# First head of a hybrid mLSTM/HGRN2 step: both halves of the key weights made in the hand-written order, the gate rows' exponentials moved among the value products, two fill steps moved between queries and scores

## The chip, the cores and the metric

The kernel runs on one core of one Trainium2 chip. The metric is device microseconds of the whole program, lower is better. The engines are named as in the profile: PE multiplies matrices (PEld loads its stationary operand), DVE, ACT and POOL work on tiles, SP issues most of the DMAs.

## The reference, cut to what matters

One layer over 32 new frames of a running stream and 512 frames of a new one (544 columns in all, 1024 features). The branch concerned here is the mLSTM branch, with four heads of 512 features:

```python
xn = _rmsnorm(h, norm_g[l]); proj = xn @ w_in[l]          # u, v, z, input and forget gates, ...
c = silu(causal_conv(u))
qm, km = c @ w_qm[h], (c @ w_km[h]) * M_HD ** -0.5        # per head, 512 x 512
lf = log_sigmoid(fg_pre + b_fg);  b = cumsum(lf)
logd = where(causal, b[t] - b[s] + ig[s], -inf)
m_t = maximum(m_prev, max(logd));  dmat = exp(logd - m_t)
s = (q @ k.T) * dmat                                       # the scores
num = w_inter * (C @ q) + s @ v                            # C, n, m are carried
hm = (layernorm(num / den) + skip * c) * silu(z);  ya = hm @ w_brm
```

The other branch (HGRN2), the merge, the output projection and a per-layer embedding follow. They are not touched.

## The kernel before, in words

Everything is float32, and every product is made of three: each operand is split into a high part `h` (ACT copies it, rounded) and a low part `l` (DVE, or POOL where `eng=G` is given, subtracts), and PE sums high·high, high·low and low·high. So a weight piece of 128x512 needs a DMA into a raw buffer (`wr`, 8 of them), an ACT copy at L132 and a subtraction at L133, and it occupies one of **five** pairs of piece buffers (`wh`/`wl`, `NPIECE`) from then until PE has read it last. `weight(...)` makes two such pieces (`wk000`, `wk001` are the two of the first half of head 0's key weights, `wk010`, `wk011` those of the second half, `wq...` those of the query weights).

The columns are worked in two halves of 272. A dense product of 128 outputs takes 24 or 48 matmuls into two PSUM buffers of a ring of four (`pd`).

**Order.** The opening of the kernel stands in a block in which PE, ACT and DVE keep the order as written: first input units, convolutions, gates, then eight rounds of value products (`vp`, L1396, round k using the pieces `wv k`), with the normalisation of the eight feature tiles (`norm` at L1287/L1290 and `norm_low` at L1294) and the splits of the next weights between them; after the rounds `value_out` empties the four value accumulators (`vh` by ACT at L1317, `vl` by DVE at L1318). After that block only PE keeps its written order. ACT, DVE, POOL and SP get their instructions from a planner that takes the earliest in program order among those it thinks ready. `tc.high_priority()` puts an instruction ahead, and `tc.issue_after(x)` keeps instructions behind x on x's engine.

**Fill.** `Pump` holds independent products (the "fill") and deals them out in steps, so that PE has work while the head's chain of dependent stages goes on. For head 0 the fill is four units `One` (z gate tiles, `wi32` to `wi35` in the profile; 4 blocks of 2 steps each) and two pairs `Two` (the next head's inputs; `wa...`, `ws...`): 60 steps in all. Block i's weights are split by `pump.prepare`, which runs `AHEAD` = 3 blocks ahead of the steps. `pump.limit` is a cap on the blocks that may be prepared. `pump.behind` makes later splits go behind a given instruction.

**Head 0 before the change.** After the rounds: values emptied, remaining norms, splits for blocks 4 and 6 (unit `wi33`), the first half of the key weights `wk00` (low parts on POOL), the last norms, and then the second step of the generator `stage_gates`: on the forget rows (4x544) a DVE operation (L726), an Exp (L727) and an Ln (L728) on ACT. Then PE runs 16 fill steps (`EARLY`: the units `wi32` and `wi33`; in them the weights of unit three, `wi34`, are split), the third step of `stage_gates` (cumulative sums and maxima on DVE, L733 to L754), `stage_k` (its second half of weights, `wk01`, is made there), the last step of `stage_gates` (Exps at L756 to L761, and the rows written to DRAM as `nm_d`), half of `stage_q`, the sums `xf_sums` for k = 0 and 3 (L329 to L341, DVE and ACT), `stage_cols` (rows turned into columns, L782), `stage_decay` (`nm_d` read back as `bc`, masks added at L804, Exp at L810 into `dm`), the other half of `stage_q`, `stage_scores` (`sc`, L881, multiplied by `dm` at L889), and `mchain`: four blocks of keys transposed (`kt`) with one fill step ahead of each, one ahead of the small transposition `kts` (L976), three more, the memory and value products (`C`, `nm`), 20 fill steps, four output transpositions (`yt`), what is left of the fill, and `stage_br` (`ya`, operands `hm`, weights `wbm`).

Of the kernel before, what the change touches and what calls it, by code (L numbers as in the profile page):

```python
# [53 lines left out]
EARLY = 16  # L54
# [12 lines left out]
def hybrid_step(ctx: ExitStack, tc: tile.TileContext, a, o):  # L67
    nc = tc.nc
    V, S, G, PE = nc.vector, nc.scalar, nc.gpsimd, nc.tensor
# [55 lines left out]
    made = {}  # L125
# [11 lines left out]
    def weight(src, name, cols=1024, eng=V, chunk=WP):  # L137

        raws = [(raw_piece(src[:, c : min(c + WP, cols)], f"{name}r{c}"), min(WP, cols - c)) for c in range(0, cols, WP)]
        return [split_piece(r, f"{name}{i}", n, chunk, eng) for i, (r, n) in enumerate(raws)]  # L140
# [157 lines left out]
    st8 = [dict(ub=[], cc=[], cs=[], vt=[], z=[]) for _ in range(MH)]  # L298
# [525 lines left out]
    def stage_k(h):  # L824

        cs = st8[h]["cs"]
        kf, ks = [], []
        for u in range(2):
            w = st8[h].pop("wk", None) or weight(a["w_km"][h, u], f"wk{h}{u}", eng=V if h else G)
            for f in range(2):  # L830
                acc = dense(w, f * P, 256, P, cs, f"k{h}{u}{f}")
                t = eslot(f"kf{h}{u}{f}")
                for b in range(2):
                    read = S.mul(t[:, half(b)], acc[b], HD**-0.5)  # L834
                if u == 0:
                    first = read
                kf.append(t)
                kh, kl = slot(f"kh{h}{u}{f}", F32R), slot(f"kl{h}{u}{f}", F32R)
                S.copy(kh[:, :NP], t[:, NS:T])
                V.tensor_tensor(kl[:, :NP], t[:, NS:T], kh[:, :NP].bitcast(F32), ALU.subtract)  # L840
                ks.append((kh, kl))
        ksm, copied = triple(kf, "ksm")
        st8[h].update(kf=kf, ks=ks, ksm=ksm, copied=copied)
        return first
# [111 lines left out]
    def mchain(h, pump):  # L956
# [5 lines left out]
        for b in range(NB):  # L962
# [7 lines left out]
                S.mul(kh[:, :HD], pt[:, 0, :], wc)  # L970
                V.scalar_tensor_tensor(kl[:, :HD], pt[:, 0, :], wc, kh[:, :HD].bitcast(F32), ALU.mult, ALU.subtract)
            kw.append((kh, kl))
        yield 4 if h else 1
        pt = paux(f"kts{h}")
        for f in range(KH):
            PE.transpose(pt[: 3 * NS, 0, f * P : (f + 1) * P], ksm[:, f], ident)  # L976
# [206 lines left out]
    def hgrn_bounds(decayed):  # L1183

        l0, l1 = vec[:, V_LB : V_LB + HH], vec[:, V_LB + HH : V_LB + 2 * HH]
        lm, le = small("lbm", [P, HH]), small("lbe", [P, 2, HH])
        V.tensor_tensor(lm, l0, l1, ALU.max)
        V.tensor_tensor(le[:, 0, :], l0, lm, ALU.subtract)
        V.tensor_tensor(le[:, 1, :], l1, lm, ALU.subtract)
        with tc.issue_after(decayed.ins):  # L1190
            S.activation(le, le, AF.Exp)

        def rest():
            V.tensor_tensor(lm, le[:, 0, :], le[:, 1, :], ALU.add)
            V.reciprocal(lm, lm)
            V.tensor_tensor(lb, le[:, 0, :], lm, ALU.mult)
            V.tensor_tensor(lc, le[:, 1, :], lm, ALU.mult)

        return rest
# [17 lines left out]
    with tc.manual_schedule(engines={mybir.EngineType.Activation, mybir.EngineType.DVE, mybir.EngineType.PE}):  # L1217
# [62 lines left out]
        def value_weight():  # L1280
            k = len(wv)
            wraw.append(raw_piece(a["w_v"][k], f"wv{k}r"))
            wv.append(split_piece(wraw[k], f"wv{k}"))

        def norm(k):
            t = xt[k]
            V.scalar_tensor_tensor(t[:, :T], t[:, :T], t[:, T : T + 1], rb[:, :T], ALU.mult, ALU.mult)  # L1287
            xh = cp.tile([P, T], F32R, name=f"xh{k}")
            xl = cp.tile([P, T], F32R, name=f"xl{k}")
            S.copy(xh, t[:, :T])  # L1290
            xs.append((xh, xl))

        def norm_low(k):
            return V.tensor_tensor(xs[k][1], xt[k][:, :T], xs[k][0].bitcast(F32), ALU.subtract)  # L1294
# [14 lines left out]
        def value_out():  # L1309
            b = len(vv0)  # L1310
            if b < 2:
                vhl = sp.tile([P, 2, SLOT], F32R, tag="d", name=f"vhl0{b}", bufs=2)
                vh, vl = vhl[:, 0], vhl[:, 1]
            else:
                vh, vl = eslot(f"vh0{b}", F32R), eslot(f"vl0{b}", F32R)
            c = r[:, b + 1 : b + 2]
            S.mul(vh[:, :HD], vp[b], c)  # L1317
            V.scalar_tensor_tensor(vl[:, :HD], vp[b], c, vh[:, :HD].bitcast(F32), ALU.mult, ALU.subtract)  # L1318
            with tc.issue_after(summed.ins):
                G.tensor_copy(vh[:, HD:VW], one4)  # L1320
                G.tensor_copy(vl[:, HD:VW], zero4)
            vv0.append((vh, vl))
# [41 lines left out]
        pump = Pump(fill(0))  # L1364
        for k in range(KD):
            if k == 1:
                conv_rest(3, uin[3], cv[3])
                silu()
                silu_low(2)
                silu()  # L1370
                fg, ig = (slot(n)[:MH, :T] for n in ("fg", "ig"))
                V.tensor_tensor(fg, gt[0:MH, :T], rb[0:MH, :T], ALU.mult)
                V.tensor_tensor(ig, gt[32 : 32 + MH, :T], rb[32 : 32 + MH, :T], ALU.mult)
                gates = stage_gates(fg, ig)
                next(gates)
                value_weight()
                silu_low(3)
                norm(0)
                norm(1)
            if k == 2:  # L1380
                value_weight()
                norm_low(0)
                norm_low(1)
                norm(2)
                value_weight()
                norm(3)
                norm_low(2)
                pump.prepare(1)
                norm_low(3)
                pump.prepare(3)  # L1390
            wh, wl = wv[k]
            xh, xl = x0[k]
            three = ((xh, wh), (xl, wh), (xh, wl))
            for b in range(NB):
                for j, (x, w) in enumerate(three):
                    PE.matmul(  # L1396
                        vp[b],
                        x[:, NS + b * P : NS + (b + 1) * P],
                        w,
                        start=(k == 0 and j == 0),  # L1400
                        stop=(k == KD - 1 and j == 2),
                    )
            if k % NB == NB - 1:
                for j in range(NB):
                    i = k + 1 - NB + j
                    PE.matmul(vq[j * NS : (j + 1) * NS, 0, :], xg[:, i], wraw[i], start=(i < NB), stop=(i >= NB))

        value_out()
        value_out()
        norm(4)  # L1410
        value_out()
        value_out()
        norm_low(4)
        norm(5)
        pump.prepare(5)
        vsum = slot("vsum")[:NS, :HD]
        S.copy(vsum, vq[:NS, 0, :])
        for j in range(1, NB):
            V.tensor_tensor(vsum, vq[j * NS : (j + 1) * NS, 0, :], vsum, ALU.add)
        pump.prepare(7)  # L1420
        st8[0]["wk"] = weight(a["w_km"][0, 0], "wk00", eng=G)
        norm_low(5)
        vs0 = small("vs", [3 * NS, VW], F32R, bufs=1)
        for i in (0, 2):
# [7 lines left out]
        norm(7)  # L1432
        norm_low(6)
        st8[0]["last"] = norm_low(7)
        next(gates)
    with tc.manual_schedule(engines={mybir.EngineType.PE}):
        for h in range(MH):
            if h:
                stage_decay(h)
            else:  # L1440
                st8[0].update(vv=vv0, vs=vs0, cc=cc, cs=cs)
                pump.to(EARLY)
                with tc.issue_after(st8[0]["copies"][0].ins):
                    next(gates)
            stage_k(h)
            if h == 0:

                st8[0]["wq"] = weight(a["w_qm"][0, 0], "wq00")
                with tc.issue_after(made["wq001"][0].ins), tc.issue_after(made["wk011"][1].ins):
                    *_, (nm_d, *rows) = gates  # L1450
            stage_q(h, 0)
            if h == 0:
                with tc.issue_after(st8[0]["last"].ins):
                    for k in (0, 3):
                        xf[k] = xf_sums(k)
                col, cols, combo = stage_cols(*rows)
                stage_decay(h)
                lower_bounds = hgrn_bounds(st8[0]["decayed"])
            low = stage_q(h, 1)
            if h == 0:  # L1460
                pump.behind = low
            else:
                pump = Pump(fill(h))
                pump.to(2)
            low = stage_scores(h)
            if h == 0:
                pump.pairs = low
                with tc.issue_after(low.ins):
                    lower_bounds()
            pump.run(mchain(h, pump))  # L1470
            pump.end()
            if h < MH - 1:
                last = stage_br(h)
            if h == 0:
                with tc.issue_after(last.ins):
                    lmask, smask = level_masks()
# [311 lines left out]
    with tc.manual_schedule(engines={mybir.EngineType.PE}):  # L1788
        pump = Pump(list(units()))
# [36 lines left out]
    for f in range(KD):  # L1826
        w = weight(a["w_brh"][f], f"wbh{f}")
# [182 lines left out]
```

## Time and profile before

| | us |
|---|---|
| median of 3 runs | 1127.63 (1126.51 to 1128.89) |
| the profiled execution, its own time | 1126.18 |
| its span, first to last instruction | 1124.3 |
| busy PE / DVE / ACT / POOL in the span | 1110.2 / 898.3 / 670.7 / 165.3 |
| mean granted TensorE clock | 0.997 |

A row of the timeline gives start, duration, engine, line, operation, output and inputs, and behind it in brackets the idle time of the engine just ahead and what ended it. `x2` is two instructions merged in one row. Matmul durations overlap, so the pace of PE is read from the starts.

### The profile page before, as it was taken

To read this page: it belongs to the slowest core of one execution; us is meant where nothing else is said; L and a number is where in the kernel's file an instruction comes from. 1 tells how busy PE (TensorE), PEld (TensorE's weight loads), DVE (VectorE), ACT (ScalarE), POOL (GpSimd) and SP (SyncE) were. 2 spreads that over 40 slices of the span, in tenths; PEclk is the share of its full clock that TensorE was granted. 3 is DMA by queue.
4 is the path that set the end of the run, shared out by engine and by line. 5 is a ranking of instruction groups with operands and counts; after the bars stand their busy time and mean duration, and the time that the engine had idled before them with its cause. 6 is when DMAs were issued, how large, how long until landed. Compare 5 with 4: busy or idle time off the path is not lost.

```text
span 1124.3 us, 23764 instructions
## 1 busy us (share of the span) xinstructions
PE 1110.2 (99%) x8733; PEld 1086.6 (97%) x8733; DVE 898.3 (80%) x2040; ACT 670.7 (60%) x1505; POOL 165.3 (15%) x308
## 2 busy tenths in 40 slices
PE   9998999999999999999999999999999999999998
PEld 8888999999999999999999999999999999999998
DVE  7888978677797685986888789999999977654485
ACT  6677446754666464665556477777676667333462
POOL 7212000100020000200110123232232210000000
PEclk9998999999999999999999999999999999999999
DMA  6133224423354132542667665666665685332753
GB/s 227 58 122 108 95 76 135 136 66 128 122 169 154 50 124 102 174 167 78 191 190 237 191 146 139 141 133 156 149 148 141 160 225 157 116 103 72 260 155 118
DMA packets 90139, 157.94 MB, mean 140 GB/s; under 512 B 10148, under 2 KB 17828, under 8 KB 90024
## 3 DMA queue, kind: packets, MB, share of 16 engines
q1 hardware_dynamic: 80352, 139.33, 38.4%
q0 software_dynamic: 8784, 15.99, 9.2%
q8 instruction: 68, 1.11, 0.4%
q10 hardware_dynamic: 888, 1.12, 0.3%
q14 instruction: 47, 0.39, 0.1%
HBM read 131.49 MB, written 24.91 MB: 139 GB/s over the span
## 4 chain that ended last, share of the span: by engine, by line
PE 90%; DVE 4%; DMA 3%; ACT 1%; issue 1%; POOL 1%; SPq 0%; ACTq 0%; POOLq 0%; DVEq 0%
PE d L502 36%; PE ya L167 8%; PE yb L167 4%; PE o L167 4%; PE pg L1857 4%; PE k L167 4%; PE q L167 4%; PE C L921 4%; PE nm L1096 3%; PE sc L881 3%; PE pl L1629 2%; PE vp L1396 2%; PE u L287 2%; DMA ws<-in_w_in 2%; PE d L387 1%
## 5 line engine op out<-in xcount | busy, mean ns | idle before, releaser
L420 POOL DMA_DIRECT2D ws<-in_w_in x46 | 40.7, 891 | 235.2 <-DVE hkq L1653 32.1
L516 ACT COPY t<-d 128x272 f32<-128x272 f32 x126 | 47.9, 380 | 8.7 <-PE d L502 8.7
L1653 DVE TENSOR_TENSOR hkq<-hkq,q 128x288 f32<-128x288 f32 (+1 forms) x96 | 40.9, 433 | 3.0 <-PE pl L1637 1.0
L1629 PE MATMUL pl<-hkq,km 128*128 128x128 f32 x224 | 37.7, 290 | 0.6 <-ACT km L1618 0.5
L651 DVE SCALAR_TENSOR_TENSOR cv<-ub,vec,cv 128x547 f32<-128x547 f32 x48 | 37.6, 784 | 0.4
L1629 PEld LDWEIGHTS pl<-hkq,km 128*128 128x128 f32 x224 | 31.1, 189 | 2.2 <-ACT km L1618 1.9
L1618 ACT COPY km<-hkq 128x256 f32<-128x256 f32 x56 | 24.1, 430 | 14.6 <-DVE hkq L1653 4.4
L1030 DVE SCALAR_TENSOR_TENSOR c<-c,wi,Cs 128x258 f32<-128x258 f32 x32 | 15.3, 479 | 18.9 <-PE Cs L1028 18.3
L933 ACT COPY Co<-C 128x258 f32<-128x258 f32 x30 | 9.8, 378 | 31.8 <-PE C L921 29.5
L1174 DVE TENSOR_TENSOR y<-ya,y 128x272 f32<-128x272 f32 x48 | 18.9, 435 | 8.7 <-PE ya L167 8.6
L1660 DVE COPY_PREDICATED at<-lmask,pl 128x256 f32<-128x256 uint8 (+1 forms) x56 | 25.3, 452 | 0.1
L643 POOL COPY uo<-ub 128x3 f32<-128x3 f32 x16 | 17.9, 1119 | 36.1 <-DVE ub L525 27.0
L1107 ACT COPY y<-nm 128x516 f32<-128x516 f32 x16 | 9.5, 591 | 22.9 <-PE nm L1096 22.4
L1597 POOL TENSOR_SCALAR_AFFINE_SELECT aa<-at 128x128 f32<-128x128 f32 x32 | 19.6, 644 | 8.1 <-DVE at L1660 8.0
L1084 DVE BATCH_NORM_STATS2 bs<-y 128x6 f32<-128x512 f32 (+1 forms) x20 | 13.8, 690 | 8.6 <-ACT y L1107 8.3
L821 POOL COPY vsm<-vt 128x96 f32<-128x96 f32 x12 | 6.8, 565 | 88.2 <-DVE vt L523 45.3
L477 POOL DMA_DIRECT2D ws<-in_w_in x15 | 15.5, 1034 | 28.5 <-DVE ws272l L133 24.2
L1096 PE MATMUL nm<-vhl,sh 128*128 128x258 f32 x112 | 18.4, 286 | 0.6 <-ACT y L1107 0.6
L1844 DVE TENSOR_TENSOR h<-o,h 128x272 f32<-128x272 f32 x16 | 6.3, 437 | 14.5 <-PE o L167 14.5
L895 ACT CAST sh<-dm 128x512 fp32r<-128x512 f32 (+3 forms) x16 | 7.4, 461 | 17.2 <-DVE dm L889 17.1
L821 POOL COPY ksm<-kf 128x96 f32<-128x96 f32 x16 | 8.5, 532 | 60.7 <-ACT kf L834 60.7
L1759 ACT ACTIVATE osq<-kq 128x128 f32<-128x128 f32 x32 | 9.8, 307 | 12.4 <-DVE kq L1754 12.1
(4495 smaller groups left out, 4996.0 us busy)
## 6 DMA issues: line engine op xcount, KB each, us to landing
ws<-in_w_in POOLq DMA_DIRECT2D x61, 256.0 KB, 4.7
ws<-in_w_in SPq DMA_DIRECT2D x46, 256.0 KB, 3.4
ya_d<-y SPq DMA_DIRECT2D x32, 272.0 KB, 2.5
y<-ya_d SPq DMA_DIRECT2D x24, 272.0 KB, 3.3
c<-in_C SPq DMA_DIRECT2D x16, 258.0 KB, 3.7
out_Cs<-c SPq DMA_DIRECT2D x16, 258.0 KB, 2.9
out_Cp<-Co SPq DMA_DIRECT2D x12, 258.0 KB, 2.4
x<-in_xT SPq DMA_DIRECT2D x8, 272.5 KB, 4.6
```

What stands on the lines that cost most here:

```text
L167: PE.matmul(both[b][:m, :TH], part(w, off + k * step, m, x), xx[:, half(b)], start=(k == 0 and j == 0), stop=(k == n - 1 and j == 2),)
L420: G.dma_start(t, w_in[u][:, i * WP : (i + 1) * WP], accum_op=ALU.add)
L502: PE.matmul(ps, ww[:, c], xx, start=(start and k == 0 and j == 0), stop=end, skip_group_check=not start,)
L516: self.kept = S.copy(t, ps)
L651: V.scalar_tensor_tensor(cv[:, :547], ub[:, j : j + 547], vcol(V_CW + 4 * ft + j), cv[:, :547], ALU.mult, ALU.add)
L881: PE.matmul(pn[:, 0, :n], ks[f][x][:, j * P : (j + 1) * P], qs[f][y][:, NS + j * P : T], start=(f == 0 and i == 0), stop=(f == KH - 1 and ...
L921: PE.matmul(pn[g][:, :VH], kw[b][x][:, f * P : (f + 1) * P], vv[b][y][:, g * VH : (g + 1) * VH], start=(b == 0 and j == 0), stop=(b == NB ...
L1096: PE.matmul(pn[:, g, :VH], st[j][x][:, (i - j) * P : (i - j + 1) * P], vv[j][y][:, g * VH : (g + 1) * VH], start=(j == 0 and q == 0), stop ...
L1629: PE.matmul(pn[:, 0, b * P : (b + 1) * P], km[:, b * P : (b + 1) * P], view(qq, b * P, ((2 * c, P // (2 * c)), (HB + c, 2), (1, c))), star ...
L1653: V.tensor_tensor(x, x, d, ALU.mult)
L1660: V.copy_predicated(at[:, :n], lmask[:, li, :n], pn[:, 0, :n])
L1857: PE.matmul(ps, part(w, k * P, P, x), xx[:, c], start=(k == 0 and j == 0), stop=(k == KD - 1 and j == 2))
```

## The change

It does five things, all for head 0.

1. The second step of `stage_gates` (L726 on DVE, Exp and Ln on ACT) is written ahead of the last value weight `wv7` in round 2, and no longer at the end of the block.
2. The splits of unit `wi33` (blocks 4 and 6) are written between the emptying of the values, ahead of `norm(4)`; the cap on the fill is then set to 8 blocks, so unit `wi34` isn't split during the 16 early steps.
3. Both halves of the key weights are made in the hand order, `wk00` after `norm(4)`, `wk01` after the sum of the short stream's values. `stage_k` finds them ready.
4. Unit `wi34`'s first piece is split after the decays (cap 9), its second after the second half of the queries; the fill then runs to step 18, which is two steps, between `stage_q` and `stage_scores`. The last step of `stage_gates` no longer stands behind `wk011`'s low part on POOL.
5. `kts` has two fill steps ahead of it and not one.

So 3 fill steps of 60 are taken earlier, and 3 fewer are left for the end of the head.

```diff
@@ stage_k
-            w = st8[h].pop("wk", None) or weight(a["w_km"][h, u], f"wk{h}{u}", eng=V if h else G)
+            w = st8[h].pop(f"wk{u}", None) or weight(a["w_km"][h, u], f"wk{h}{u}", eng=V if h else G)
@@ mchain, ahead of kts
-        yield 4 if h else 1
+        yield 4 if h else 2
@@ value rounds, k == 2
                 norm(2)
+                next(gates)
                 value_weight()
@@ after the rounds
         value_out()
         value_out()
-        norm(4)
+        pump.prepare(5)
         value_out()
         value_out()
+        pump.prepare(7)
+        pump.limit = 8
+        norm(4)
+        st8[0]["wk0"] = weight(a["w_km"][0, 0], "wk00", eng=G)
         norm_low(4)
         norm(5)
-        pump.prepare(5)
...
-        pump.prepare(7)
-        st8[0]["wk"] = weight(a["w_km"][0, 0], "wk00", eng=G)
+        st8[0]["wk1"] = weight(a["w_km"][0, 1], "wk01", eng=G)
         norm_low(5)
...
         st8[0]["last"] = norm_low(7)
-        next(gates)
@@ head loop, h == 0
-                with tc.issue_after(made["wq001"][0].ins), tc.issue_after(made["wk011"][1].ins):
+                with tc.issue_after(made["wq001"][0].ins):
                     *_, (nm_d, *rows) = gates
...
                 lower_bounds = hgrn_bounds(st8[0]["decayed"])
+                pump.limit = 9
+                pump.prepare(9)
             low = stage_q(h, 1)
             if h == 0:
+                pump.limit = None
                 pump.behind = low
+                pump.to(EARLY + 2)
```

## The prediction

> **What bounds the kernel now.** I read the page first, then the waits of PE in head 0, then PE's timeline where those waits lie.
>
> ```profile
> PE 1110.2 (99%) x8733; PEld 1086.6 (97%) x8733; DVE 898.3 (80%) x2040; ACT 670.7 (60%) x1505; POOL 165.3 (15%) x308
> ```
> ```profile
> PE k L167 <- POOL wk011l L133: 2.2, 1, 2.2
> PE k L167 <- ACT wk011h L132: 1.1, 1, 1.1
> PE sc L881 <- ACT q L860: 0.9, 1, 0.9
> PE d L387 <- DVE wi330l L133: 0.9, 1, 0.9
> PE kts L976 <- DVE kwl L971: 0.4, 1, 0.4
> ```
>
> PE carries the span, so only its idle time, and time at a lower clock, can be won. The second fence is all that PE waited for between 55 and 130 us: five waits, 5.5 us, and the change touches each of them. What they really cost is read from the starts:
>
> ```profile
> 62.09 0.77 PE L387 MATMUL d<-x,wi320h 128*128 128x272 f32 x4
> ...
> 68.23 0.66 PE L387 MATMUL d<-x,wi330h 128*128 128x272 f32 x4
> ...
> 75.38 0.41 PE L167 MATMUL k<-cs0h,wk000h 128*128 128x272 f32 x2
> ...
> 81.40 0.42 PE L167 MATMUL k<-cs0h,wk010h 128*128 128x272 f32 x2
> ...
> 84.19 0.52 PE L167 MATMUL k<-cs2h,wk011h 128*128 128x272 f32 x2 [1.12 <-ACT wk011h L132]
> 84.55 0.42 PE L167 MATMUL k<-cs2l,wk011h 128*128 128x272 f32 x2
> 87.20 0.82 PE L167 MATMUL k<-cs2h,wk011l 128*128 128x272 f32 x2 [2.24 <-POOL wk011l L133]
> 87.82 0.66 PE L167 MATMUL k<-cs3h,wk011h 128*128 128x272 f32 x2
> ...
> 92.81 0.56 PE L167 MATMUL k<-cs2h,wk011l 128*128 128x272 f32 x2
> ...
> 93.96 0.42 PE L167 MATMUL q<-cs0h,wq000h 128*128 128x272 f32 x2
> ...
> 107.68 0.63 PE L881 MATMUL sc<-q,kh 128*128 128x512 f32 x2
> ...
> 109.07 0.62 PE L881 MATMUL sc<-q,kh 128*128 128x512 f32 x2
> ...
> 110.81 0.97 PE L881 MATMUL sc<-q,kh 128*128 128x512 f32 x2 [0.89 <-ACT q L860]
> ...
> 123.78 0.64 PE L976 MATMUL kts<-ident,ksm 128*96 128x128 f32 x4 [0.45 <-DVE kwl L971]
> ```
> ```profile
> 87.40:94.00 6.60, 6.60 (x33) 6.60 (x34) 5.15 (x18) 2.92 (x6) 0.93 (x2) 0.57 0.26 82
> ```
>
> The first half of the keys takes 81.40 − 75.38 = 6.02 us, the second, with the same matmuls, 93.96 − 81.40 = 12.56: 6.54 us too long. Some 3.4 of that is waiting for `wk011`; the rest is that the eleven groups from 87.82 to 92.81 are 0.454 us apart, where the first half's twenty-four are 6.02/24 = 0.251, and the table by stage gives a granted clock of 0.57 there. So this wait is paid almost twice.
>
> **The change part by part.** *What goes.* (a) Unit 33 takes 75.38 − 68.23 = 7.15 us, unit 32 68.23 − 62.09 = 6.14: 1.01 us, if unit 33's weights are split between the values. (b) 6.54 us of the second key half. (c) The score wait: 0.89, and 0.97 − 0.62 = 0.35 for the slow pair behind it: 1.24. Two fill steps now lie there:
>
> ```profile
> 170.07 9.04 PE d L502 x72
> ```
>
> These are twelve steps, 0.753 us each, so two last 1.5 us, and cover the wait. (d) One step more ahead of `kts` covers its 0.45. Sum: 1.01 + 6.54 + 1.24 + 0.45 = 9.24 us. The 60 steps are the same work in other places, so they cost nothing themselves.
>
> Is (b) safe? `wk010` and `wk011` now get the piece buffers of units 32 and 33, which PE gives up half through unit 33, and `wi34` takes none. A low part on POOL takes between
>
> ```profile
> 76.81 1.30 POOL L133 TENSOR_TENSOR wk010l<-wk01r,wk010h 128x512 fp32r<-128x512 f32 x1 [4.71 <-ACT wk010h L132]
> ...
> 84.28 2.87 POOL L133 TENSOR_TENSOR wk011l<-wk01r,wk011h 128x512 fp32r<-128x512 f32 x1
> ```
>
> 1.30 and 2.87 us (the long one beside busy DVE), and no longer stands behind the copies of `ksm` there. Freed some 4 us before the keys begin, and first needed 6 us into them, they have over 5 us to spare. In SP's queue `wk01`'s loads move ahead of `wi4`'s, which PE wants only after 150 us; the fill's raws that come later leave the query weights' way. ACT's hand order now stands at `wk011h` until unit 33 has given up a piece; behind it wait two value scalings and the last two norms, which only the next stages' sums need, and DVE has the value sums and the gate rows meanwhile. I take zero; were the cover gone, 2 us of ACT.
>
> *What comes: exponentials among the values.* ACT and DVE keep the order as written there, and pass work to and fro:
>
> ```profile
> 54.71 0.65 ACT L1290 CAST xh<-x 128x544 fp32r<-128x544 f32 x1 [2.73 <-DVE x L1287]
> 55.27 0.62 ACT L132 CAST wv7h<-wv7r 128x512 fp32r<-128x512 f32 x1
> ```
> ```profile
> 78.88 1.28 ACT L727 ACT_TABLE_LOAD   x1
> 80.17 0.66 ACT L727 ACTIVATE row<-row 4x544 f32<-4x544 f32 x1
> 80.74 0.37 ACT L834 ACTIVATE kf<-k 128x272 f32<-128x272 f32 x1
> 81.12 1.28 ACT L728 ACT_TABLE_LOAD   x1
> 82.42 0.66 ACT L728 ACTIVATE row<-row 4x544 f32<-4x544 f32 x1
> 82.98 0.65 ACT L834 ACTIVATE kf<-k 128x272 f32<-128x272 f32 x2
> ```
>
> Exp and Ln each bring a table load: (80.74 − 78.88) + (82.98 − 81.12) = 3.72 us, now between the two rows of the first fence. So `wv7h` starts at 58.99 and not at 55.27. Queued behind it on ACT: the cast of `norm(3)`, both pieces of unit 32, the value copies; on DVE, which waits for `wv7h`: `wv7l`, the norms, unit 32's low parts, the value subtractions. PE waits twice:
>
> ```profile
> 58.20 0.63 PE L1396 MATMUL vp<-wv7h,x 128*128 128x512 f32 x2
> ```
> ```profile
> 60.51 1.41 DVE L1318 SCALAR_TENSOR_TENSOR vhl<-vp,rms_r,vhl 128x512 fp32r<-128x512 f32 x2
> ```
>
> first for `wv7h` (ready near 59.6 where it is wanted at 58.20), and then, as unit 32 needs the buffers of the first two values, for the subtractions that end at 61.92 now and 3.72 later then. Unit 32 starts at 62.09 now, 0.17 behind them; so it starts 3.72 − 0.17 = 3.55 us later. That is my value; the nearest rows bound it by 0 (the 2.73 us for which ACT stood ahead of 54.71, if the norm came sooner) and 3.72.
>
> The Trainium skill (*ScalarE: Activation LUTs*, "Table sets: the hidden batching unit") says that Exp and Ln share a set and need one load. The trace differs: two loads, 1.28 each; by that rule the delay would be 2.4 in place of 3.72 and the total 1.3 lower. The same page ("What ACT_TABLE_LOAD costs") adds a drain of 1.38 us to every switch; here Exp starts 1.29 us after its load does, so no run shows that drain, and by it the total would be 2.8 higher.
>
> A further load, back to Silu for the first gate tile near 71 us, is 1.28 on ACT that PE waits for nowhere, as the four PSUM buffers of units 32 and 33 are emptied by DVE; at most 1.28.
>
> *What comes: unit 34's first piece late.* Its low part is now behind the decays in program order, and the two steps ahead of the scores need it. PE reaches them at 107.68 − 1.01 − 6.54 + 3.55 = 103.68. When is DVE there?
>
> ```profile
> 60.40:107.70 47.30, 43.09 (x322) 40.92 (x321) 41.31 (x87) 33.62 (x71) 11.43 (x16) 0.93 0.39 124
> ```
> ```profile
> 106.68 0.88 DVE L804 TENSOR_TENSOR dm<-bc,cmask 128x128 f32<-128x128 f32 x4
> ```
>
> From the last piece of unit 32 (60.4) to the decays' masks and what is with them (107.7) DVE is busy for 41.3 of 47.3 us. The same list, less `wi341l` and L726 (0.6 each), is 40.1 us, and begins 3.72 later, at 64.1: it ends at 104.2 without idle time, at 110.2 with all of the 6 us idle now. Part of that idle time was for `wi33`, the emptying of the values and `wq`, which waited for things that come earlier now; I keep 1 to 2 us. `wi340l` is near the end of the list, or fills a gap in it: between 0 and 3 us of waiting on PE (6 in the rival below). I take 1.0, nearer to zero since the planner can put it where the decays still wait for their DMA.
>
> The rows themselves are no limit: Exp and Ln are done 24 us sooner, the rest follows after the first gate tile, and their columns are wanted 4 us earlier than now.
>
> *The tail.* Three steps fewer stand ahead of `ya`: 2.26 us.
>
> ```profile
> 177.19 0.69 DVE L133 TENSOR_TENSOR wbm001l<-wbm00r,wbm001h 128x512 fp32r<-128x512 f32 x1
> ```
> ```profile
> 180.47 0.41 PE L167 MATMUL ya<-hm2h,wbm001h 128*128 128x272 f32 x2
> ```
>
> `wbm001l` ends at 177.88 and is wanted at 180.47: 2.59 us of cover, 0.33 left. Zero; if the order on DVE slips, under 1 us.
>
> **Sum**: 9.24 − 3.55 − 1.0 = 4.7 us less. The profiled execution's 1126.18 would be 1121.5. It is 1.45 under the median of the runs, so the median goes from 1127.63 to 1122.9. About 0.2%, 2.3 us, is what a measurement of this kernel can tell from no change.
>
> **The rivals.**
>
> *DVE becomes the bound (slower).* The decays' masks came at 106.68 since DVE had a queue. If it keeps its idle time, as PE's earlier arrival doesn't shorten its list, everything slips by 3.72: masks near 110.4, `wi340l` behind them, done at 111.1. Then PE stands from 103.68 on for 7.4 us instead of 1.0: 4.7 − 6.4 = 1.7 us slower, and with `kts`' wait left (0.45) and a tail slip of 0.6, 2.7: 1130.4. It decides from `wi340l` at 109.4 on (103.68 + 1.0 + 4.7). For it: in the last stage ahead of the scores DVE is busy for 7.53 of 7.60 us.
>
> ```profile
> 100.00:107.60 7.60, 7.60 (x71) 7.42 (x70) 7.53 (x23) 6.03 (x16) 1.26 (x5) 1.00 0.36 112
> ```
>
> Against it: several of its waits were for pieces that are now early.
>
> *The clock drops among the values.* PE would idle 1.4 us near 58 and 2 us near 64, with 3 us of work between. The trace shows that 1.12 and 2.24 us with 0.8 of work between took the clock to 0.57 for 5 us; the extra was 11 × (0.454 − 0.251) + 0.4 at its ends, 2.6 us. That puts the time at 1125.5. Against it: 0.89 and 0.85 us alone did nothing, and the work between is four times as long. The Trainium skill (*TensorE: Matmul & The Clock Gate*, "Part 1: The HAM clock gate") wants an idle window of about 3.4 us for this. By that rule nothing drops here; but the row at 87.20 dropped after 2.24 us in one piece, so the trace leaves it possible.
>
> *The exponentials fit into the gaps.* ACT stood for 2.73 us ahead of 54.71. If most of the 3.72 us is hidden, 3 us come back: 1119.9. Against it: the order as written puts them behind the cast at 54.71, whose input comes from DVE.
>
> *It doesn't do what it says.* `wk011`'s piece is asked for while five are in use; if ACT's stop at it holds up what DVE needs, the wait is moved to the start of the keys, and (b) yields perhaps 2 of 6.54: 1127.4, no change. Against it: 5 us to spare.
>
> **How the numbers follow.** Forecast 60%, DVE the bound 12%, clock 10%, fitting gaps 10%, no effect 8%. The forecast's own range, from the ends of the costs (`wi340l` 0 to 3, `kts` unmended), is 1121.9 to 1125.3. For 8 in 10 I take in the fitting gaps, the clock drop and part of the no-change case: 1119.5 to 1126.7. Faster by over 0.2%: forecast, gaps, and most of the clock case, 0.77; within: 0.10; slower: 0.13.
>
> **What would show it.** No wait of PE for `wk010`, `wk011` or `wi33`, both key halves near 6.0 us at full clock; the table loads L727 and L728 near 55 to 58 us, `wv7h` near 59, the first matmul of unit 32 near 65.6; the scores starting near 106 with no wait inside, `kts` without one. I am wrong if unit 32 starts below 63.5 or above 67, if the two steps ahead of the scores wait over 3 us, or if the granted clock is under 0.9 anywhere from 58 to 72.

## The result and the profile after

| | before | after |
|---|---|---|
| median of five runs, us | 1128.08 (1126.51 to 1129.05) | 1133.43 (1132.39 to 1134.52) |
| the profiled execution, own time / span, us | 1126.18 / 1124.3 | 1132.39 / 1130.5 |

The ratio is 1.0049 (95%: 1.0034 to 1.0064): the change makes the kernel slower by about 5.4 us. The forecast was 4.7 us faster. The median of the kernel before was 1128.08 here, 1126.69 beside the first four experiments and 1126.90 beside the other four, so the experiments are compared by their ratios.

PE still carries the span (first part of the page of after), and the waits of PE between 55 and 205 us show what it stood for (total, times, longest):

```profile
PE 1112.0 (98%) x8733; PEld 1087.1 (96%) x8733; DVE 895.3 (79%) x2040; ACT 670.6 (59%) x1506; POOL 169.2 (15%) x308
```
```profile
PE ya L167 <- ACT hm2h L105: 4.6, 1, 4.6
PE vp L1397 <- ACT wv7h L132: 1.5, 1, 1.5
PE d L387 <- DVE vhl L1318: 1.3, 2, 1.1
PE nm L1042 <- DMA c<-in_C: 1.2, 1, 1.2
PE sc L881 <- ACT q L860: 0.8, 1, 0.8
```

The waits for `wk011`, `wi330l` and `kwl` are gone. The second and third lines are the price forecast for the Exp and Ln. The first and fourth are new, the first alone is about as long as the whole forecast gain, and no step of the prediction has either. The timeline of PE after, at the places that were shown of before:

```profile
65.25 0.39 PE L387 MATMUL d<-x,wi320h 128*128 128x272 f32 x1 [1.06 <-DVE vhl L1318]
...
71.91 0.67 PE L387 MATMUL d<-x,wi330h 128*128 128x272 f32 x4
...
77.94 0.41 PE L167 MATMUL k<-cs0h,wk000h 128*128 128x272 f32 x2
...
83.97 0.42 PE L167 MATMUL k<-cs0h,wk010h 128*128 128x272 f32 x2
...
90.48 0.41 PE L167 MATMUL q<-cs0h,wq000h 128*128 128x272 f32 x2
...
105.55 0.62 PE L881 MATMUL sc<-q,kh 128*128 128x512 f32 x2
...
108.60 0.98 PE L881 MATMUL sc<-q,kh 128*128 128x512 f32 x2 [0.81 <-ACT q L860]
```

The queries start 3.48 us earlier than before (90.48 against 93.96). The table places the gain and the loss; each entry is the start of the stage's first matmul on PE, in us; the last column is the span from first to last instruction.

| kernel | unit 32 | keys | queries | scores | `kts` | `C` | `ya` | keys of head 1 | span |
|---|---|---|---|---|---|---|---|---|---|
| before | 62.1 | 75.4 | 94.0 | 107.7 | 123.8 | 128.9 | 179.0 | 203.0 | 1124.3 |
| after | 65.2 | 77.9 | 90.5 | 105.6 | 121.7 | 130.0 | 177.4 | 208.3 | 1130.5 |
| e1_c0_first | 65.2 | 77.9 | 90.5 | 105.6 | 121.7 | 126.8 | 174.1 | 205.8 | 1127.5 |
| e2_conv_behind | 65.1 | 77.8 | 90.4 | 105.4 | 121.6 | 129.9 | 177.3 | 201.8 | 1123.9 |
| e3_both | 65.2 | 77.9 | 90.4 | 105.5 | 121.6 | 126.7 | 174.1 | 198.6 | 1119.8 |
| e4_exp_behind | 62.2 | 74.4 | 87.2 | 103.1 | 119.7 | 124.8 | 172.1 | 196.6 | 1118.1 |
| e5_exp_old | 62.2 | 74.4 | 88.4 | 104.1 | 119.1 | 124.1 | 171.5 | 195.9 | 1117.1 |
| e6_qf | 62.7 | 74.9 | 87.7 | 103.5 | 118.4 | 123.4 | 170.7 | 195.3 | 1118.1 |
| e7_kts_one | 65.4 | 78.1 | 90.8 | 105.9 | 121.3 | 126.4 | 175.1 | 203.7 | 1125.1 |
| e8_steps_back | 65.3 | 78.0 | 90.6 | 104.2 | 123.2 | 128.3 | 178.4 | 202.5 | 1123.9 |

From the keys of head 1 to the end every kernel takes 921.2 to 922.8 us: what the change does is decided by then. At `kts` PE of after is 2.10 us earlier and has three fill steps more behind it, 2.26 us by the row of twelve steps: 4.4 us ahead. From there on it loses. `kts` to `C` takes 8.37 us where it took 5.11 (121.68 to 130.05 against 123.78 to 128.89): 3.26 lost. `C` to `ya` is 2.73 shorter, 2.26 of it the three steps that lie elsewhere: 0.47 won. `ya` to the keys of head 1 takes 30.91 where it took 24.00: 6.91 lost. 4.36 − 3.26 + 0.47 − 6.91 is −5.34, the distance between 202.96 and 208.30.

**Loss A, the first memory products.** PE's first products with the memory `c`, first before, then after; then, from the queue of SP, the loads of `c`, again before and after:

```profile
126.61 0.64 PE L1042 MATMUL nm<-c,qw 128*32 128x258 f32 x8
```
```profile
125.76 2.65 PE L1042 MATMUL nm<-c,qw 128*32 128x258 f32 x8 [1.21 <-DMA c<-in_C]
```
```profile
93.49 1.00 SPq L986 DMA_DIRECT2D c<-in_C  x2
122.28 0.80 SPq L986 DMA_DIRECT2D c<-in_C  x2
```
```profile
121.90 1.85 SPq L986 DMA_DIRECT2D c<-in_C  x4
```

Eight matmuls that took 0.64 us before take 2.65, behind a wait of 1.21. The granted clock is 1.00 there (124 to 130 us), so the slow pace is not the clock's; that the four loads land one after the other fits it. All four loads are issued at 121.90; before, two of them were at 93.49. The tiles `c0` come from the same ring of twelve buffers (`eslot`) as the gate tile that each `One` unit leaves (`gate_one`). Unit `wi34` ends with step 24 of the fill. Before, 16 + 4 + 1 = 21 steps stood ahead of `kts`, behind which the loads are written; now there are 18 + 4 + 2 = 24. So the gate tile of `wi34` is now ahead of the loads in program order, and takes a buffer that was theirs.

**Loss B, the end of the head.** PE after, at `ya`, and the stage's windows (start:end, length, then busy time and instructions of PE, PEld, DVE, ACT and POOL, granted clock, DMA share, GB/s):

```profile
183.66 0.52 PE L167 MATMUL ya<-hm2h,wbm001h 128*128 128x272 f32 x2 [4.61 <-ACT hm2h L105]
184.51 0.82 PE L167 MATMUL ya<-hm2l,wbm001h 128*128 128x272 f32 x2 [0.33 <-DVE hm2l L106]
185.13 0.65 PE L167 MATMUL ya<-hm2h,wbm001l 128*128 128x272 f32 x2
185.58 0.66 PE L167 MATMUL ya<-hm3h,wbm001h 128*128 128x272 f32 x2
```
```profile
183.60:187.80 4.20, 3.80 (x17) 3.59 (x17) 3.77 (x6) 2.15 (x7) 0.00 (x0) 0.59 0.16 57
```

The wait is 4.61 + 0.33, and the groups behind it come at a pace of 0.454 us (185.13, 185.58, 186.04) in place of 0.251, at a granted clock of 0.59: 6.9 us together. What ACT did instead of `hm2h`, before and after:

```profile
175.35 0.65 ACT L105 CAST hm2h<-c 128x544 fp32r<-128x544 f32 x1
...
176.58 0.65 ACT L105 CAST hm3h<-c 128x544 fp32r<-128x544 f32 x1
...
178.44 0.84 ACT L646 ACTIVATE cv<-ub,vec 128x547 f32<-128x547 f32 x1
```
```profile
176.86 0.85 ACT L646 ACTIVATE cv<-ub,vec 128x547 f32<-128x547 f32 x1
...
181.64 0.23 ACT L657 ACTIVATE c<-cv 128x32 f32<-128x32 f32 x1 [3.42 <-DVE cv L651]
...
182.42 0.65 ACT L105 CAST cs4h<-c 128x544 fp32r<-128x544 f32 x1
182.97 0.64 ACT L105 CAST hm2h<-c 128x544 fp32r<-128x544 f32 x1
183.52 0.64 ACT L105 CAST hm3h<-c 128x544 fp32r<-128x544 f32 x1
```

L646, L657 and `cs4h` are the convolution of the next head, which the fill itself starts (`inner`) once its first tile is complete, at step 50. Before, the four outputs `hm` were written at steps 45 to 48, ahead of it. With three steps fewer left they come at steps 48 to 51, and the convolution is ahead of `hm2` and `hm3`. ACT stands 3.42 us for the convolution's own input with the two copies for which PE waits queued behind it.

### The profile page after: what moved, and what is told of

Same layout as the page of the kernel before. It is cut to its first block, busy times and chain, and to the rows that moved or that the text cites. A ratio compares the mean times of both kernels' runs of the same rounds, so it can differ in the third digit from the quotient of the medians.

```text
span 1130.5 us, 23774 instructions
## 1 busy us (share of the span) xinstructions
PE 1112.0 (98%) x8733; PEld 1087.1 (96%) x8733; DVE 895.3 (79%) x2040; ACT 670.6 (59%) x1506; POOL 169.2 (15%) x308
## 3 DMA queue, kind: packets, MB, share of 16 engines
q10 hardware_dynamic: 888, 1.12, 0.3%
## 4 chain that ended last, share of the span: by engine, by line
PE 90%; DVE 5%; DMA 2%; ACT 2%; issue 1%; SPq 0%; POOL 0%; ACTq 0%; DVEq 0%
PE d L502 37%; PE ya L167 8%; PE pg L1863 4%; PE yb L167 4%; PE o L167 4%; PE q L167 4%; PE C L921 4%; PE k L167 4%; PE nm L1096 3%; PE sc L881 3%; PE pl L1635 2%; PE u L287 2%; PE vp L1397 1%; PE ple L167 1%; PE d L387 1%
## 5 line engine op out<-in xcount | busy, mean ns | idle before, releaser
L821 POOL COPY vsm<-vt 128x96 f32<-128x96 f32 x12 | 7.3, 607 | 87.7 <-DVE vt L523 45.3
L1837 DVE TENSOR_TENSOR gb<-yb,gb 128x272 f32<-128x272 f32 x16 | 6.3, 435 | 13.1 <-PE yb L167 13.1
```

## The experiments

All are the kernel after with the edits shown. The theory: losses A and B are separate consequences of the three moved steps in program order, and what the prediction costed otherwise holds. Rivals: the loss comes from the exponentials' place, or from one slip that shows twice.

**e1_c0_first** writes the four loads of head 0 ahead of the fill steps at `kts`.

```diff
+        if h == 0:
+            c0 = [eslot(f"c0{h}{f}") for f in range(KH)]
+            for f in range(KH):
+                nc.sync.dma_start(c0[f][:, :VW], a["C0"][h, f])
         yield 4 if h else 2
...
-        c0 = [...]; loads
+        if h:
+            c0 = [...]; loads
```

> The changed kernel with the four state tiles c0 of head 0 asked for, and their loads issued, ahead of the fill steps in front of kts and not behind kts. Theory A: with two steps there, unit 34 is finished first, its output tile comes ahead of c0 in the ring of twelve, and the loads of c0 wait for it (issued at 121.9, two of them at 93.5 before). Then two loads go out near 92 to 98, the wait of the first sample products (1.2 us, and the slow pace behind it, 3.4 in all) shrinks to 0 to 1.5 us, the time falls by 2 to 3.4: 1130.0 to 1131.4. Rival: the ring is full or SP's queue is held by other loads anyway; then the loads still go out behind 120 us and the time stays at 1133.4.

1129.67 us, ratio to before 1.0027 (1.0018 to 1.0036). The loads on SP:

```profile
88.59 1.19 SPq L976 DMA_DIRECT2D c<-in_C  x2
120.03 0.80 SPq L976 DMA_DIRECT2D c<-in_C  x2
```

Two are early again, PE waits for no `c`, and `kts` to `C` takes 5.09 us, as before the change. That is 3.3 us. `ya` still waits 4.6 us for `hm2h`:

```profile
180.39 0.82 PE L167 MATMUL ya<-hm2h,wbm001h 128*128 128x272 f32 x2 [4.61 <-ACT hm2h L105]
```

The slow groups behind this wait go on for longer than in after (the last section), so 2.5 of the 3.3 us are left at the keys of head 1. So A is its own loss.

**e2_conv_behind** writes the convolution behind the four outputs.

```diff
@@ inner
-            if f == 0:
+            if f == 0 and h:
                 conv(h + 1)
@@ after the splits of hm, h == 0
+            if h == 0:
+                conv(1)
```

> The changed kernel with one thing moved: the next head's first convolution is written behind the four output splits of head 0 (after the last output transposition) and not where the fill ends its first input tile. Same instructions, same fill steps. Theory A (program order): in the changed kernel three more fill steps are done when the outputs come, so the tile that starts the convolution (step 50) is finished ahead of the third output and not behind the fourth, and the planner puts hm2h and hm3h behind the convolution's SiLU on ACT. Then ya's wait for hm2h (4.61 us) and its slow clock go, 6.9 us in all: about 1126.5. Rival (cover): the three steps taken from the tail (2.26 us) were what hid the output splits; then the wait for hm2h stays at 4 us or more and the time stays at 1133.4.

1125.72 us, ratio 0.9991 (0.9982 to 0.9999). ACT and PE at that place:

```profile
176.74 0.65 ACT L105 CAST hm2h<-c 128x544 fp32r<-128x544 f32 x1
...
177.91 0.64 ACT L105 CAST hm3h<-c 128x544 fp32r<-128x544 f32 x1
178.46 0.84 ACT L646 ACTIVATE cv<-ub,vec 128x547 f32<-128x547 f32 x1
```
```profile
180.11 0.52 PE L167 MATMUL ya<-hm3l,wbm001h 128*128 128x272 f32 x2 [0.18 <-DVE hm3l L106]
```

The wait of 4.61 and the slow clock are gone, `ya` to the keys of head 1 takes 24.6 us (24.0 before the change), and the keys of head 1 come 6.5 us earlier. The wait for `c` stays (1.3 us). So B is its own loss and the larger.

**e3_both** has both edits.

> Both moves together. Theory A: the costs are separate places on PE's path and add: 1133.4 - 6.9 - (2 to 3.4) = 1123.1 to 1124.5, below the kernel before (1128.1) by 3.6 to 5. Rival: DVE is the bound from the queries to ya, so that what is won early is waited for later: not under 1126.

1121.68 us, ratio 0.9954 (0.9941 to 0.9966): 5.2 us faster than before, where the forecast was 4.7. (The median is 1.4 below the range expected here; that of the kernel before was 1.4 lower too, 1126.69 against 1128.08.) Without B, the move of the loads is worth its whole price: the keys of head 1 come 3.2 us earlier than in e2_conv_behind.

**e4_exp_behind** is e3_both with Exp and Ln written behind the splits of `wi33`, ahead of `norm(4)`.

```diff
                 norm(2)
-                next(gates)
                 value_weight()
...
         pump.limit = 8
+        next(gates)
         norm(4)
```

> As the kernel with both moves, and the Exp and Ln of the gate rows are written behind the emptying of the values and the splits of unit 33 (ahead of norm(4)), no longer ahead of wv7. Theory A (3.7 us of ACT among the values cost PE 3.5): unit 32 starts near 62.2 and not 65.9, PE has no wait for wv7h or the values, and the time is 3 to 3.7 under that kernel: about 1120. Rival: ACT's 3.7 us then hold up the key weights or the norms instead; PE waits at the first keys (from 74 us on), and less than 1.5 us is won.

1119.94 us, ratio 0.9933 (0.9920 to 0.9947). Unit 32 starts at 62.2, 3.0 us earlier than in e3_both, and the keys 3.5 us earlier: the forecast price of the exponentials among the values (3.55) is real. Only 2.0 us are left at the keys of head 1: PE waits 0.6 for `kf` at the first queries and 1.1 in the scores.

**e5_exp_old** is e3_both with Exp and Ln in their old place, the end of the hand-ordered block.

```diff
                 norm(2)
-                next(gates)
                 value_weight()
...
         st8[0]["last"] = norm_low(7)
+        next(gates)
```

> The kernel with both moves, and the Exp and Ln of the gate rows at their place of before (end of the hand order, behind the last norm). Unit 32 starts near 62.2, as with the Exps behind the values. Theory A (the early place is needed, since PE now comes to the rows' columns at about 93 us and the rows, from an Exp near 79 on, need till 96 or 97): PE waits 2 to 4 us at the columns or the scores, 1122 to 1124. Rival (the rows were held only by the order behind wk011): no wait there, 1120, as with the Exps behind the values.

1120.74 us, ratio 0.9936 (0.9923 to 0.9949), not to be told from e4_exp_behind. The rows did not need an earlier place than they had: PE waits for them nowhere. Exp and Ln still cost something where they stand, as the `kf` that PE waits for in the keys comes on ACT behind Ln's table load (at 80.09) and Ln (at 81.38):

```profile
82.37 0.39 PE L167 MATMUL k<-cs0h,wk010h 128*128 128x272 f32 x1 [1.69 <-ACT kf L834]
```

**e6_qf** is e4_exp_behind with the copy `qf` (L857) in `tc.high_priority()`, as the cast behind it already was.

```diff
-            S.copy(t["qf"][:, i * NS : (i + 1) * NS], acc[0][:, :NS])
+            with tc.high_priority():
+                S.copy(t["qf"][:, i * NS : (i + 1) * NS], acc[0][:, :NS])
```

In after, ACT's queue ahead of the late scores reads:

```profile
107.78 0.31 ACT L811 ACTIVATE dm<-dm,cols 96x32 f32<-96x32 f32 x1
107.99 0.20 ACT L1191 ACTIVATE lbe<-lbe 128x16 f32<-128x16 f32 x1
108.10 0.17 ACT L857 COPY qf<-q 128x32 f32<-128x32 f32 x1
108.16 0.38 ACT L860 CAST q<-q 128x272 fp32r<-128x272 f32 x1
```

The cast for which the scores wait is behind `qf`, and `qf` behind the decays' Exps, which begin at 104.84.

> The kernel with the Exps behind the values, and the copy of the short stream's queries (L857) put ahead like the casts beside it. Theory A (the score wait is ACT's queue: the last half's cast stands behind that copy, and the copy behind the ten Exps of the decays; fill steps on PE can't cover what ACT does 3 us later): the wait of 1.1 us and the slow pair behind it go, 1.0 to 1.5 us less: 1118.5 to 1119. Rival (the decays themselves are late): the wait moves to the first product with dm, no gain.

1117.84 us, ratio 0.9919 (0.9906 to 0.9933). ACT now, and PE, which has no wait in the scores:

```profile
102.44 0.17 ACT L858 COPY qf<-q 128x32 f32<-128x32 f32 x1
102.52 0.67 ACT L861 CAST q<-q 128x272 fp32r<-128x272 f32 x2
...
104.02 1.28 ACT L810 ACTIVATE dm<-bc,col 128x128 f32<-128x128 f32 x4
```

From the keys to the keys of head 1 it takes 120.4 us against 122.2 in e4_exp_behind. The interval of the ratio overlaps that of e4_exp_behind, so the gain at the end is probable, and the removal of the wait is shown. The span in the table doesn't show the gain: the profiled execution took 1119.99, and from the keys of head 1 to the end, which no edit here touches, it is 1.3 us slower than that of e4_exp_behind (922.8 against 921.5). This is the fastest version of the study, some 9 us under the kernel before.

**e7_kts_one** and **e8_steps_back** test the count of steps itself. e7_kts_one gives `kts` one step again, so 23 stand ahead of the loads; e8_steps_back takes the two ahead of the scores back as well.

```diff
-        yield 4 if h else 2
+        yield 4 if h else 1
@@ e8_steps_back only
-                pump.to(EARLY + 2)
```

> The changed kernel with one step ahead of kts and not two, nothing else. Unit 34 then ends (step 24) behind c0's place in the program, and the next head's first input tile (step 50) is finished ahead of the fourth output and not of the third. Theory A: c0's loads go out before 100 us and its 3.4 us are gone; hm2h is early, and ya waits for hm3h in the place of hm2h: still 2.5 to 5 us of waiting, with a slow clock behind it if it is over 2: 1127 to 1130. Rival (cover): one step moved back to the tail gives 0.75 us of 4.61: ya still waits for hm2h.

e7_kts_one: 1127.12 us, ratio 0.9998 (0.9989 to 1.0007). Its loads, and PE at `ya`:

```profile
88.95 1.17 SPq L986 DMA_DIRECT2D c<-in_C  x2
120.43 0.80 SPq L986 DMA_DIRECT2D c<-in_C  x2
```
```profile
179.75 0.52 PE L167 MATMUL ya<-hm3h,wbm001h 128*128 128x272 f32 x2 [2.28 <-ACT hm3h L105]
```

One step less and A is gone whole (5.11 us from `kts` to `C`), though nothing else was done for the loads: unit `wi34` now ends behind them. B is smaller by the one output that is ahead of the convolution again: the wait is for `hm3h` and not `hm2h`, 2.28 us and not 4.61, and ACT has `hm2h` at 171.73, `L646` at 172.80 and `hm3h` at 179.06. That is what the count of steps asks for.

> The changed kernel with parts 4 and 5 undone as far as fill steps go: none between queries and scores, one ahead of kts. The key weights, the splits of unit 33 and the Exps among the values stay as changed. Theory A (all that the change lost behind the scores came from being three steps further when the head's tail is written): loads of c0 out before 100 us, hm2h and hm3h ahead of the next head's convolution, no wait of ya over 0.5 us; the time is the two gains less the values, 1.0 + 6.5 - 3.6 = 3.9 below the kernel before (1126.7): about 1122.8, within 1 us of the kernel with both moves (1121.7). Rival (the steps are worth what the prediction gave them, 1.24 + 0.45): 1.7 us above that kernel or more, 1123.4 to 1125.

e8_steps_back: 1125.86 us, ratio 0.9986 (0.9977 to 0.9995): neither A nor B, but 3 us above the theory's 1122.8. The rival (the steps are worth what the prediction gave them) is nearer, and it too stopped lower, at 1125. PE and the stage's window, then ACT's last cast ahead of these scores, before the change and here:

```profile
108.73 0.97 PE L881 MATMUL sc<-q,kh 128*128 128x512 f32 x2 [2.30 <-ACT q L860]
```
```profile
108.70:114.00 5.30, 5.27 (x20) 4.89 (x21) 2.39 (x4) 2.15 (x4) 0.23 (x2) 0.68 0.44 136
```
```profile
110.38 0.39 ACT L860 CAST q<-q 128x272 fp32r<-128x272 f32 x1
```
```profile
108.30 0.37 ACT L860 CAST q<-q 128x272 fp32r<-128x272 f32 x1
```

PE comes to the scores 3.5 us earlier than before the change, ACT's last cast only 2.1 (108.30 against 110.38). So the wait grows from 0.89 to 2.30 and takes the clock with it: scores to `kts` take 19.0 us against 16.1. By the starts, from the keys to the scores 6.1 us are won, the keys themselves begin 2.6 later, and the scores lose 2.9: 0.5 is left at the keys of head 1. So the two steps ahead of the scores do pay.

## Why the prediction was wrong

- **The tail: the step that failed.** The sum rests on "The 60 steps are the same work in other places, so they cost nothing themselves". As work they are the same; in other places they changed the order of what stands around them, and both losses come from that. For the tail the prediction has "Zero; if the order on DVE slips, under 1 us". It costs 6.9 us. I measured the slack of `wbm001l` in the order as it stood, and took that order as given; three steps fewer ahead of `ya` put the convolution ahead of two of the four outputs, on ACT. e2_conv_behind takes the loss away and e7_kts_one halves the wait, so this is shown.
- **The step ahead of `kts`: a term missing.** It was costed as a gain of 0.45, which it gave (`kts` has no wait in after). What it finishes as the third of the moved steps, a unit whose output takes a buffer, stood in no part of the sum: 3.3 us. e1_c0_first and e7_kts_one show it from two sides: the place in program order decides. That it does so through the ring of buffers is read from the program; which earlier tile each load waits for stays open.
- **(c), the score wait: a cover that did not cover.** I counted 1.24 us as won, without asking what on ACT holds up the cast that the scores wait for. The wait went from 0.89 to 0.81. It hangs on ACT, where `qf` stands behind the decays' Exps, and PE's earlier arrival lengthens it: without the two steps it is 2.30 (e8_steps_back). The two steps kept it from growing; e6_qf removed it. (It is gone in e5_exp_old too, where PE comes to the scores 1.0 us later than in e4_exp_behind.)
- **Right in kind and size.** (a) unit 33 takes 6.03 us and not 7.15: 1.12, forecast 1.01. (b) the second key half takes 6.51 and not 12.56: 6.05, forecast 6.54; the rest is one pair that comes 0.23 us late at 87.21 and takes 0.26 longer. The values: unit 32 starts 3.16 later, forecast 3.55, and with the second wait, inside unit 32, unit 33 starts 3.68 later; e4_exp_behind gives 3.5 back at the keys. (d) as forecast.
- **`wi340l`: costed at 1.0, measured 0.** Its low part ran at 96.68, and PE wants it at 104.5.
- **The sum up to `kts`** was right within 0.3 us: 4.4 us ahead, forecast 4.7 in all. e3_both confirms it with 5.2 us at the end. That it is so near is in part luck: about 0.8 us too much in (c) and 0.5 in (b) are balanced by the 1.0 of `wi340l` that never came.
- **The rivals.** The slower one had the sign but not the mechanism: DVE did not bind. The clock did not drop among the values: it is 1.00 from 57 to 66 us with idle times of 1.47 and 1.06. The Exps did not fit into gaps (unit 32 is 3.2 us later). What happened was in none of them; the 13% for slower were for something else.
- **The signs of being wrong.** None of the three came true: unit 32 started at 65.25, between 63.5 and 67; the two steps ahead of the scores did not wait; and the clock was 1.00 from 58 to 72 us. All three look at places ahead of the scores, and both losses lie behind them.

## What to carry to other kernels

When steps of independent work are moved, list what each step also emits: the tile that it finishes, the buffer that this takes, and the follow-up work that it starts. Each of these changes its place in program order against everything written near it, and a planner that goes by program order will put it ahead of what used to come first. Slack measured in the old order says nothing about that. A stage reached earlier is a gain only if the queue that feeds it gets earlier by as much: in e8_steps_back ACT came 2.1 us earlier where PE came 3.5.

## What the runs showed of the hardware

How long may PE stand before its clock falls? Alone, 1.47 us (after, ahead of the last values) and 1.69 us (e5_exp_old) left it at 1.00; the third number from the end of a window is the granted clock:

```profile
57.00:66.00 9.00, 6.21 (x29) 3.33 (x27) 5.51 (x9) 7.52 (x13) 0.00 (x0) 1.00 0.16 39
```
```profile
83.00:88.00 5.00, 5.00 (x43) 5.00 (x42) 5.00 (x11) 2.97 (x9) 3.79 (x3) 1.00 0.40 114
```

2.28 us (e7_kts_one) and 2.30 us (e8_steps_back) took it down, to 0.68 from 108.7 to 114.0 in the second, as shown above, and in the first to 0.64:

```profile
179.50:184.20 4.70, 4.12 (x18) 3.90 (x19) 3.35 (x5) 1.64 (x5) 0.00 (x0) 0.64 0.49 165
```

Between 1.69 and 2.28 us no run has a wait that stands alone. What the slow stretch costs on top of the wait doesn't follow the wait's length. From `ya` to the keys of head 1, after lost 6.9 us with 4.61 + 0.33 of waiting and e7_kts_one 4.6 (28.6 against 24.0) with 2.28 + 0.33: 2.0 on top in both, at the same pace of 0.454 us for some 4 us. But e1_c0_first, with the same 4.61 as after, lost 7.7 (31.7 against 24.0), 3.1 on top: its slow groups go on until 186.3, and the granted clock from 180.3 to 186.3 is 0.52. In the kernel before, 1.12 and 2.24 us close together had 3.2 on top (6.54 less 3.36). In e8_steps_back the scores lost 2.9, 1.4 of it longer waiting: 1.5 on top. So in these runs a wait of over 2 us cost 1.5 to 3.2 us more than itself; what sets the amount stays open.

The Trainium skill (*TensorE: Matmul & The Clock Gate*, "Part 1: The HAM clock gate") gives an idle window of about 3.4 us ahead of the drop. The slow stretch behind 4.61 us agrees with it; those behind 2.28 and 2.30 us do not, and here the measurement decides.
